# Up projections of both feed-forward stages: eight block products before, seven after

## The chip, the cores and the metric

The kernel runs on one core of a Trainium2 chip. Times are device microseconds (us); the kernel before was run three times, and its profile is one further execution. TensorE (PE) does the matrix products, VectorE (DVE), ScalarE (ACT) and GpSimd (POOL) the elementwise work, and SyncE (SP) issues the transfers. Each of them takes its instructions in order.

## The reference

One decoder layer on 512 tokens of width 1024: a feed-forward half step, a mixer of two kinds of attention, an attention into a memory, and a second feed-forward half step, each with a residual and a layer norm. The change concerns the two feed-forward stages, with weights of their own:

```
h = layer_norm(alpha*h + 0.5 * (silu(h @ w1) * (h @ w3)) @ w2)   # w1, w3: 1024 x 2816, w2: 2816 x 1024
```

Everything is float32.

## The kernel before

Tokens are kept transposed in `hT`: 1024 channels as eight contraction tiles of 128, 512 tokens along the free dimension. The 2816 hidden channels are 22 "f-tiles" of 128. An f-tile needs a piece of w1 and a piece of w3, [128, 1024] each (eight contraction tiles side by side), and for the down product a piece of w2, also [128, 1024].

A float32 operand is kept as two parts of twelve bits, `hi` and `lo`, in the type fp32r. `split` makes them: a cast gives `hi`, on ACT or DVE, whichever the planner expects to end first; a subtract on DVE, the source less `hi`, gives `lo`. Each product is then three matmuls (`mm3`, line 260): hi with hi, hi with lo, lo with hi. `project` forms one column tile of h @ w: eight contraction tiles, 24 matmuls of 512 columns into one PSUM bank.

The f-tiles form ten groups: nine of two, and the last of four. `ffn` issues the up products of group g + 1, then the down products of group g: for each of four token tiles and two halves of the output a bank `res`, which DVE adds to the accumulator `acc`. So a round of the loop is four up projections (96 matmuls) and 48 matmuls of the down product. `gated` turns two finished up banks into the gate g: silu on ACT, a multiply on DVE, and a split. The first group of the second stage goes through `project_halves`, token half by token half, since the norm before it releases the tokens in tiles; each norm is followed by PE's transposes `trh`, whose banks are split into `hT`.

Weights pass through `Weights` (from line 272): a transfer into one of three raw buffers, then a split into one of five `hl` buffers. A piece is asked for when an earlier one is done with, so the split of the piece waits until PE has read the old content of its buffer. Gates, accumulators, norm constants and other tiles of 4 KB a partition share an arena of 20 slots; there are seven work tiles [128, 512] and eight PSUM banks.

The order of the instructions is made by a planner (`Issue`): generators issue PE's instructions, and an instruction of another engine leaves when the planner's clock says that its data should be there. Splits of weights carry a delay (`LATER`, 4 us), by which they give way to others. On the chip each engine runs its queue in the order so made. In names below, `w1_1_8` is the piece of w1 for stage 1, f-tile 8; the second feed-forward stage has the number 4.

Of the kernel before, what the change touches and what calls it, by code (L numbers as in the profile page):

```python
# [10 lines left out]
F32 = mybir.dt.float32  # L11
# [7 lines left out]
P = 128  # L19
# [24 lines left out]
class Op:  # L44
    """An instruction that awaits its turn: a form for each engine that could run it."""
# [6 lines left out]
class Mark:  # L52
    """The time from which awaited data can be read; endless until it is set and the last instruction before it left."""
# [9 lines left out]
class Issue:  # L63
    """Sets the order of the instructions. Generators issue the tensor engine's; each yields what its next piece waits
    for (nothing, a Mark, or a condition), and of those that could go on the one of the highest rank does. The clock
    counts the rows of the tensor engine. The other engines' instructions are charged by their size and leave when what
    they read should be there, so that none holds up its engine's queue."""
# [46 lines left out]
    def first(self):  # L114
        """Of the pending instructions that could start soonest, the one whose data and delay say so."""
# [5 lines left out]
    def delayed(self, ns):  # L121
        """Instructions in here give way to those whose data came up to ns later, or the other way round."""
# [4 lines left out]
    def set(self, mark, *aps):  # L127
        """The mark for these tiles as they will be after what has left or is pending."""
# [33 lines left out]
def form(engine, name, op, args, kw):  # L162
    """Engine, nanoseconds on it and after it, call; then what the call writes and reads."""
# [15 lines left out]
class Timed:  # L179
    """An engine whose instructions await their turn."""  # L180
# [12 lines left out]
def layer(ctx: ExitStack, tc: tile.TileContext, a: dict, out: bass.AP):  # L193
# [20 lines left out]
    def bank(name):  # L214
        """A bank of PSUM; what still reads one that was dropped leaves first when all are taken."""
# [12 lines left out]
    def drop(*tiles):  # L228
        """Nothing issued from here on reads these banks."""
# [10 lines left out]
    def scaled(out, src, scale=None):  # L240
        """out = src * scale on ScalarE or VectorE, whichever ends first."""
# [15 lines left out]
    def matmul(ps, w, x, start, stop):  # L257
        issue.pe(lambda: nc.tensor.matmul(ps, w, x, start=start, stop=stop), ps, w, x)  # L258

    def mm3(ps, w, x, first, last):  # L260
        """(w0 + w1).T @ (x0 + x1) without the product of the two low parts, which lies below float32's last bit."""
        matmul(ps, w[0], x[0], first, False)
        matmul(ps, w[0], x[1], False, False)
        matmul(ps, w[1], x[0], False, last)
# [7 lines left out]
    class Weights:  # L272
        """Pieces of up to 1024 columns in the order of their use, as two parts of twelve bits whose sum they are;
        up to `depth` are on chip or on their way."""
# [7 lines left out]
        def fetch(self):  # L282
            key, src = self.specs.pop(0)
            n = src.shape[1]
# [25 lines left out]
    # ---------------------------------------------------------------- constants  # L310
# [19 lines left out]

    def first_loads():
        """The first weights and x, in pieces that let the products start."""
# [3 lines left out]
        for k0, k1, x0, x1 in ((0, 2, 0, 1), (2, 4, 1, 2), (4, 8, 2, 4), (8, 8, 4, 6), (8, 8, 6, 8)):  # L336
# [3 lines left out]
            raw = slot(f"xT{x0}", F32)  # L340
            raw = raw[:, :x1 - x0]
# [9 lines left out]
    def project(name, w, toks=slice(None), o=0):  # L351
        """A column tile of h @ w, transposed: [128 channels, tokens] in a bank."""
# [7 lines left out]
    def project_halves(keys, ready):  # L360
        """Column tiles of h @ w on half of the tokens, then on the other half, each when its norm is done."""
# [110 lines left out]
    def plan_ffn(n, w1, w3, w2):  # L472
# [6 lines left out]
        for g, fs in enumerate(groups):  # L479
            if g + 1 < len(groups):  # L480
                up(groups[g + 1])
# [747 lines left out]
```

## Time and profile before

| | us |
|---|---|
| median of three runs (1301.07 to 1302.55) | 1301.34 |
| profiled execution: span | 1300.1 |
| PE busy in the span | 1279.1 |
| DVE busy | 736.5 |
| ACT busy | 403.7 |
| first feed-forward stage, products from | 10.38 |
| second stage, products from | 924.08 |

The span is the profiled program from its first to its last instruction; the runs are timed from outside. The share of busy time is an average over stages with different limits, so a stage is read by its own stretch: the chain of waits, which follows the work that ended last back from the end, shows in each stretch the engine that was waited for. A matmul's mean duration in the groups is longer than the distance from one to the next, since they are pipelined; durations of DVE and ACT overlap a little too.

### The profile page before, as it was taken

What the parts mean: (1) busy time and instruction counts of PE and PEld (TensorE: products, weight loads), DVE (VectorE), ACT (ScalarE), POOL (GpSimd) and SP (SyncE); (2) the same over time, 40 slices, a digit from 0 to 9 for tenths busy, and PEclk for the clock granted to TensorE, in tenths of its full rate; (3) what the DMA queues carried; (4) which work ended last, traced back from release to release, by engine and by line L of the source; (5) the groups of instructions that cost most, each with busy time, mean ns of one, the idle gap of its engine ahead of it and who ended that gap; (6) DMA issues with size and microseconds to landing.
All of it is one profiled execution on the core that took longest, in us unless ns stands there. A gap on an engine that the chain in (4) does not pass through costs nothing.

```text
span 1300.1 us, 15614 instructions
## 1 busy us (share of the span) xinstructions
PE 1279.1 (98%) x6210; PEld 1059.8 (82%) x6210; DVE 736.5 (57%) x1250; ACT 403.7 (31%) x670; POOL 22.8 (2%) x33
## 2 busy tenths in 40 slices
PE   7999999999999999999999999999999999999997
PEld 5888887888889987877778898888988888888886
DVE  5444444354482799666657684574754444444446
ACT  3122222121133476334441253451422222222211
POOL 0000000000010000000000000000100000000000
PEclk9999999999999999999999999999999999999999
DMA  7323333243332412232333444234532232332231
GB/s 272 127 97 97 98 97 91 66 146 98 114 110 91 133 50 66 64 115 81 97 98 113 169 171 147 81 125 151 196 124 89 94 97 98 97 97 87 94 96 65
DMA packets 43212, 142.99 MB, mean 110 GB/s; under 512 B 4963, under 2 KB 6755, under 8 KB 43140
## 3 DMA queue, kind: packets, MB, share of 16 engines
q1 hardware_dynamic: 43140, 142.00, 33.6%
q8 instruction: 49, 0.80, 0.3%
q14 instruction: 23, 0.19, 0.0%
HBM read 132.94 MB, written 9.04 MB: 109 GB/s over the span
## 4 chain that ended last, share of the span: by engine, by line
PE 92%; DVE 5%; ACT 1%; DMA 1%; issue 1%; SPq 0%; POOL 0%; DVEq 0%; POOLq 0%; ACTq 0%
PE pw L258 38%; PE res_w L258 18%; PE mq L258 3%; PE res_w_o L258 3%; PE pgd L258 3%; PE res_mem_w_o L258 2%; PE mk L258 2%; PE vd L258 2%; PE qd L258 2%; PE pw_gm L258 2%; PE kd L258 2%; PE mv L258 2%; PE pyd L258 2%; PE cq L258 1%; PE pgm L258 1%; DVE ed L176 1%
## 5 line engine op out<-in xcount | busy, mean ns | idle before, releaser
L258 PE MATMUL pw<-hT,w_hl 128*128 128x512 f32 (+1 forms) x2208 | 502.5, 388 | 6.9 <-DVE w_hl L176 4.7
L258 PEld LDWEIGHTS pw<-hT,w_hl 128*128 128x128 f32 x2208 | 403.8, 189 | 101.8 <-ACT hT L176 7.5
L176 ACT CAST w_hl<-w_raw 128x1024 fp32r<-128x1024 f32 x129 | 133.5, 1050 | 514.5 <-PE pw L258 326.4
L176 DVE TENSOR_TENSOR w_hl<-w_raw,w_hl 128x1024 fp32r<-128x1024 f32 (+1 forms) x134 | 160.0, 1205 | 156.1 <-ACT w_hl L176 155.9
L258 PE MATMUL res_w<-w_hl,g 128*128 128x512 f32 x1056 | 243.3, 390 | 0.0
L258 PEld LDWEIGHTS res_w<-w_hl,g 128*128 128x128 f32 x1056 | 198.0, 188 | 41.8 <-DVE w_hl L176 0.3
L176 DVE TENSOR_TENSOR acc<-acc,res_w 128x512 f32<-128x512 f32 x128 | 85.3, 685 | 50.4 <-PE res_w L258 50.4
L176 DVE SCALAR_TENSOR_TENSOR s<-pw,s 128x512 f32<-128x512 f32 x44 | 30.4, 691 | 141.3 <-PE pw L258 140.6
L258 PE MATMUL pgd<-hT,w_gd_hl 128*128 128x512 f32 x192 | 47.5, 400 | 0.0
L258 PE MATMUL mq<-hT,mem_wq_hl 128*128 128x512 f32 x192 | 46.1, 398 | 0.0
L258 PE MATMUL res_mem_w_o<-mem_w_o_hl,moT 128*128 128x512 f32 x192 | 44.5, 391 | 0.0
L258 PE MATMUL res_w_o<-w_o_hl,zT 128*128 128x512 f32 x192 | 44.5, 391 | 0.0
L258 PEld LDWEIGHTS mq<-hT,mem_wq_hl 128*128 128x128 f32 x192 | 35.8, 188 | 8.3
L258 PEld LDWEIGHTS pgd<-hT,w_gd_hl 128*128 128x128 f32 x192 | 35.5, 188 | 8.4
L258 PEld LDWEIGHTS res_mem_w_o<-mem_w_o_hl,moT 128*128 128x128 f32 x192 | 35.8, 188 | 7.7 <-DVE mem_w_o_hl L176 0.3
L258 PEld LDWEIGHTS res_w_o<-w_o_hl,zT 128*128 128x128 f32 x192 | 35.8, 188 | 7.7 <-DVE w_o_hl L176 0.3
L176 ACT ACTIVATE s<-pw 128x512 f32<-128x512 f32 x44 | 26.0, 591 | 16.6 <-PE pw L258 16.6
L176 POOL TENSOR_TENSOR rs_ln<-ms_ln,mhalf 128x1 f32<-128x1 f32 x16 | 13.4, 836 | 997.7 <-DVE ms_ln L176 997.7
L176 DVE TENSOR_TENSOR g<-s,g 128x512 fp32r<-128x512 f32 x44 | 30.1, 684 | 0.0
L176 DVE SCALAR_TENSOR_TENSOR acc<-acc,res_w 128x512 f32<-128x512 f32 x32 | 21.6, 684 | 13.2 <-PE res_w L258 13.2
L176 ACT ACTIVATE sq<-acc,nmu 128x1024 f32<-128x1024 f32 x16 | 18.5, 1154 | 30.7 <-DVE nmu L176 29.2
L258 PE MATMUL pgm<-hT,w_gm_hl 128*128 128x512 f32 x96 | 24.9, 402 | 0.0
(243 smaller groups left out, 1397.1 us busy)
## 6 DMA issues: line engine op xcount, KB each, us to landing
w_raw<-in_ffn_w SPq DMA_DIRECT2D x131, 512.0 KB, 3.6
h_dram<-acc SPq DMA_DIRECT2D x12, 512.0 KB, 2.7
acc<-h_dram SPq DMA_DIRECT2D x12, 512.0 KB, 5.8
w_gm_raw<-in_w_gate SPq DMA_DIRECT2D x8, 512.0 KB, 3.5
w_gd_raw<-in_w_gate SPq DMA_DIRECT2D x8, 512.0 KB, 3.5
w_o_raw<-in_w_o SPq DMA_DIRECT2D x8, 512.0 KB, 3.5
mem_wk_raw<-in_mem_wk SPq DMA_DIRECT2D x8, 512.0 KB, 4.1
mem_wq_raw<-in_mem_w_q SPq DMA_DIRECT2D x8, 512.0 KB, 4.1
```

What stands on the lines that cost most here:

```text
L176: return (name, ns, 1500.0 if name == "sync" else 0.0, lambda: getattr(engine, op)(*args, **kw)), outs, ins
L258: issue.pe(lambda: nc.tensor.matmul(ps, w, x, start=start, stop=stop), ps, w, x)
```

## The change

The f-tiles 2 to 21 of each stage are taken in ten pairs, and the up projections of a pair as a product of 2 x 2 blocks: two f-tiles (f0, f1), two halves of the contraction (K0, K1) and two halves of the tokens (one, two). Each block of weights, b0 = (f0, K0), b1 = (f1, K0), b2 = (f0, K1), b3 = (f1, K1), is [128, 1024]: 512 columns of w1 and 512 of w3. `up` is hT's first half of contraction tiles, `low` its second. The seven products, in their order of issue, each with 24 matmuls of 256 columns into one bank:

```
P1 = b0 . up[one]            P5 = (b0+b1) . a           P6 = (b0+b1+b3) . b      P3 = b3 . c
P7 = (b1+b3) . (up[one]-up[two])    P2 = b2 . low[one]    P4 = (b0+b1+b3+b2) . low[two]
a = low[two]-up[two]    b = -a-up[one]    c = -b-low[one]
bank x: P1, then P6, P7, P4 on top;   bank z: P5, then P3 on top;   bank y: P2
f0[one] = P1+P2   f0[two] = x after P4   f1[one] = -(x after P6 + z)   f1[two] = -(P5 + x after P7)
```

ACT copies bank x after P1, bank z after P5 and bank x after P6 (tiles p1, p5, u2), and DVE adds to these what is still missing; the signs are taken in by the scale of silu and of the multiply. The four sums of h are split into four tiles once per stage (`sums_of_h`), two of them in the pool `ppool` that the mixer uses between the stages. The sums of weights are formed in place in the raw blocks by DVE, each before its split. Blocks now lie in the arena and come in two transfers of 256 KB. For the sums, the raw x is kept (first stage), or ACT copies the transposes of the norm's output (second stage, 16 copies). The first group of each stage goes as before; after it `ffn` waits by a mark for the sums of h.

```diff
-    def mm3(ps, w, x, first, last):
+    def mm3(ps, w, x, first, last, again=False):
...
         def fetch(self):
             key, src = self.specs.pop(0)
+            if callable(src):
+                hl = wsplit.tile([P, 2, 1024], F32R, tag="hl", name=f"{key}_hl")
+                with issue.delayed(LATER):
+                    src(hl)
+                self.tiles[key] = hl
+                self.held += 1
+                return
...
                 split(dst[:, :, 0], dst[:, :, 1], ps.rearrange("p (k t) -> p k t", k=4))
+                if n == 3:
+                    for j in range(2):
+                        act.copy(h_raw[2 * half + j][:, :, t * P:(t + 1) * P], ps[:, j * 256:(j + 1) * 256].rearrange("p (k t) -> p k t", k=2))
...
+        def load(self, *blocks):
+            for i in blocks:
+                if i not in self.b:
+                    self.b[i] = slot(f"{self.name}_b{i}", F32, [P, 1024])
+                    for w, src in enumerate(self.src):
+                        sp.dma_start(self.b[i][:, w * 512:w * 512 + 512], src[i % 2][:, i // 2 * 512:i // 2 * 512 + 512])
...
+        def make(self, i, hl):
+            b = self.b
+            if i == 1:
+                self.load(0, 1, 3, 2)
+            if self.after and i in (3, 2):
+                self.after.load(*((0, 1) if i == 3 else (3, 2)))
+            for at, other in {5: ((0, 1),), 6: ((0, 3),), 7: ((1, 3),), 4: ((0, 2),)}.get(i, ()):
+                SUM.tensor_tensor(b[at], b[at], b[other], op=ALU.add)
+            src = b[{1: 0, 5: 0, 6: 0, 4: 0, 3: 3, 7: 1, 2: 2}[i]]
+            split(hl[:, 0], hl[:, 1], src)
...
+    ORDER = (1, 5, 6, 3, 7, 2, 4)
+    SUM = dve
...
+        with issue.delayed(LATER):
+            for j in range(2):
+                up, low = h_raw[j], h_raw[2 + j]
+                kk = slice(2 * j, 2 * j + 2)
+                a, b, c = [wk(f"S{n}_{j}{i}").rearrange("p (k t) -> p k t", k=2) for i in "abc"]
+                dve.tensor_tensor(a, low[:, :, two], up[:, :, two], op=ALU.subtract)
+                split(views[0][:, kk, 0], views[0][:, kk, 1], a)
+                dve.scalar_tensor_tensor(b, a, -1.0, up[:, :, one], op0=ALU.mult, op1=ALU.subtract)
+                split(views[1][:, kk, 0], views[1][:, kk, 1], b)
+                dve.scalar_tensor_tensor(c, b, -1.0, low[:, :, one], op0=ALU.mult, op1=ALU.subtract)
+                split(views[j][:, 4:6, 0], views[j][:, 4:6, 1], c)
+                dve.tensor_tensor(a, up[:, :, one], up[:, :, two], op=ALU.subtract)
+                split(s3[j][:, :, 0], s3[j][:, :, 1], a)
...
+        def seven(p):
...
+            def product(ps, i, first):
+                hl = W.take(f"wp{n}_{p}_{i}")
+                for w in range(2):
+                    for k in range(4):
+                        o = w * 512 + k * P
+                        mm3(ps[:, w * 256:(w + 1) * 256], hl_of(hl, slice(o, o + P)), sums[i](k),
+                            first and w == 0 and k == 0, w == 1 and k == 3, not first)
+                W.done(f"wp{n}_{p}_{i}")
+
+            def out(dst, c, sign):
+                act.activation(dst, c[:, :256], AF.Silu, scale=sign)
+                dve.scalar_tensor_tensor(dst, c[:, 256:], 0.5 * sign, dst, op0=ALU.mult, op1=ALU.mult)
...
+            product(x, 1, True)
+            p1 = wk(f"p1_{n}_{p}")
+            act.copy(p1, x)
+            yield
+            z = bank(f"pz{n}_{p}")
+            product(z, 5, True)
+            p5 = wk(f"p5_{n}_{p}")
+            act.copy(p5, z)
+            yield
+            product(x, 6, False)
+            u2 = wk(f"u2_{n}_{p}")
+            act.copy(u2, x)
+            yield
+            product(z, 3, False)
+            dve.tensor_tensor(u2, u2, z, op=ALU.add)
+            drop(z)
+            out(gw[1][:, one], u2, -1.0)
+            yield
+            product(x, 7, False)
+            dve.tensor_tensor(p5, p5, x, op=ALU.add)
+            out(gw[1][:, two], p5, -1.0)
+            gT[f1] = slot(f"g{n}_{f1}")
+            split(gT[f1][:, 0], gT[f1][:, 1], gw[1])
+            yield
+            y = bank(f"py{n}_{p}")
+            product(y, 2, True)
+            dve.tensor_tensor(p1, p1, y, op=ALU.add)
...
+            product(x, 4, False)
+            out(gw[0][:, two], x, 1.0)
...
             if g + 1 < len(groups):
-                yield from up(groups[g + 1])
+                for f in groups[g + 1][::2]:
+                    yield from seven(f // 2)
             yield from down(g)
```

The change moves instructions on PE and on DVE. PE's queue in a round of the first stage, before: the up products of f-tile 8 and the start of f-tile 9 (`pw1`, `pw3` are the banks of w1 and w3, `hT0` and `hT1` the two halves of the contraction).

```order
L258 MATMUL res1_w2_1_4_3_1_893<-w2_1_5_hl_732,g1_5_627 128x512 x3
L258 MATMUL pw1_1_8_910<-hT0_89,w1_1_8_hl_762 128x512 x12
L258 MATMUL pw1_1_8_910<-hT1_90,w1_1_8_hl_762 128x512 x12
L258 MATMUL pw3_1_8_942<-hT0_89,w3_1_8_hl_798 128x512 x12
L258 MATMUL pw3_1_8_942<-hT1_90,w3_1_8_hl_798 128x512 x12
L258 MATMUL pw1_1_9_974<-hT0_89,w1_1_9_hl_828 128x512 x12
```

After, the pair of f-tiles 10 and 11 (`px`, `pz`, `py` are the banks x, z, y of pair 5; `wp1_5_6` is the block of product 6; `S1`, `S3` hold the sums of h).

```order
L258 MATMUL px1_5_1566<-hT0_89,wp1_5_1_hl_1412 128x256 x24
L258 MATMUL pz1_5_1603<-S1_0_114,wp1_5_5_hl_1444 128x256 x24
L258 MATMUL px1_5_1566<-S1_1_115,wp1_5_6_hl_1476 128x256 x24
L258 MATMUL pz1_5_1603<-S1_0_114,wp1_5_3_hl_1551 128x256 x6
L258 MATMUL pz1_5_1603<-S1_1_115,wp1_5_3_hl_1551 128x256 x6
...
L258 MATMUL px1_5_1566<-S3_1_0_116,wp1_5_7_hl_1554 128x256 x6
L258 MATMUL px1_5_1566<-S3_1_1_117,wp1_5_7_hl_1554 128x256 x6
...
L258 MATMUL py1_5_1726<-hT1_90,wp1_5_2_hl_1591 128x256 x24
L258 MATMUL px1_5_1566<-hT1_90,wp1_5_4_hl_1628 128x256 x24
```

Four projections of 24 wide matmuls became seven products of 24 narrow ones; three take tokens from `hT`, four from the tiles of sums, and bank x is written four times.

DVE's queue in a round, before: from the low parts of a piece of w3 and two of w2 to that of f-tile 12's w3 (names ending in `hl` are split weights, `raw` the loaded ones, `s` and `g` the gate).

```order
L176 TENSOR_TENSOR w3_1_11_hl_1107<-w3_1_11_raw_1106,w3_1_11_hl_1107 128x1024
L176 TENSOR_TENSOR w2_1_8_hl_1109<-w2_1_8_raw_1108,w2_1_8_hl_1109 128x1024
L176 TENSOR_TENSOR w2_1_9_hl_1144<-w2_1_9_raw_1143,w2_1_9_hl_1144 128x1024
L176 SCALAR_TENSOR_TENSOR s1_10_1178<-pw3_1_10_1148,s1_10_1178 128x512
L176 CAST g1_10_1179<-s1_10_1178 128x512
L176 TENSOR_TENSOR w1_1_12_hl_1174<-w1_1_12_raw_1173,w1_1_12_hl_1174 128x1024
L176 TENSOR_TENSOR g1_10_1179<-s1_10_1178,g1_10_1179 128x512
L176 TENSOR_TENSOR w3_1_12_hl_1210<-w3_1_12_raw_1209,w3_1_12_hl_1210 128x1024
```

After, from the end of pair 4's product 3 on (`wp1_5_b0` is pair 5's raw block b0, into which the sums go; `gw` is the gate before its split).

```order
L176 CAST wp1_5_1_hl_1412<-wp1_5_b0_1245 128x1024
L176 TENSOR_TENSOR p5_1_4_1322<-p5_1_4_1322,px1_4_1259 128x512
L176 TENSOR_TENSOR wp1_5_1_hl_1412<-wp1_5_b0_1245,wp1_5_1_hl_1412 128x1024
L176 SCALAR_TENSOR_TENSOR gw1_4_1_1258<-p5_1_4_1322,gw1_4_1_1258 128x256
L176 TENSOR_TENSOR wp1_5_b0_1245<-wp1_5_b0_1245,wp1_5_b1_1246 128x1024
L176 CAST g1_9_1413<-gw1_4_1_1258 128x512
L176 CAST wp1_5_5_hl_1444<-wp1_5_b0_1245 128x1024
L176 TENSOR_TENSOR p1_1_4_1287<-p1_1_4_1287,py1_4_1419 128x512
L176 TENSOR_TENSOR wp1_5_5_hl_1444<-wp1_5_b0_1245,wp1_5_5_hl_1444 128x1024
L176 TENSOR_TENSOR g1_9_1413<-gw1_4_1_1258,g1_9_1413 128x512
L176 TENSOR_TENSOR wp1_5_b0_1245<-wp1_5_b0_1245,wp1_5_b3_1285 128x1024
L176 SCALAR_TENSOR_TENSOR gw1_4_0_1257<-p1_1_4_1287,gw1_4_0_1257 128x256
```

The gate of one pair and the weight blocks of the next now alternate instruction by instruction, and casts and additions of 1024 stand among the subtracts.

PE's queue where the second stage begins, before (`trh3_3` are the transposes of the last token tile, `pw1_4_0` the first bank of the stage).

```order
L258 MATMUL pw3_4_0_7585<-hT0_89,w3_4_0_hl_7547 128x256 x12
L258 MATMUL pw3_4_0_7585<-hT1_90,w3_4_0_hl_7547 128x256 x12
L258 MATMUL pw1_4_1_7586<-hT0_89,w1_4_1_hl_7549 128x256 x12
L258 MATMUL pw1_4_1_7586<-hT1_90,w1_4_1_hl_7549 128x256 x12
L258 MATMUL pw3_4_1_7587<-hT0_89,w3_4_1_hl_7551 128x256 x12
L267 MATMUL trh3_3_0_7685<-ident_84,acc3_3_7227 128x128 x4
L267 MATMUL trh3_3_1_7690<-ident_84,acc3_3_7227 128x128 x4
```

After, at the same place.

```order
L258 MATMUL pw3_4_0_8650<-hT0_89,w3_4_0_hl_8602 128x256 x12
L258 MATMUL pw3_4_0_8650<-hT1_90,w3_4_0_hl_8602 128x256 x12
L258 MATMUL pw1_4_1_8651<-hT0_89,w1_4_1_hl_8604 128x256 x12
L267 MATMUL trh3_3_0_8729<-ident_84,acc3_3_8270 128x128 x4
L267 MATMUL trh3_3_1_8734<-ident_84,acc3_3_8270 128x128 x4
```

The transposes moved ahead of 24 of the 84 matmuls that stood before them.

DVE's queue there, after (`S4_0` and so on are the sums of h of that stage, `hraw` the raw transposes; `w1_4_1` belongs to the first group, which goes as before).

```order
L176 TENSOR_TENSOR wp4_1_b1_8609<-wp4_1_b1_8609,wp4_1_b3_8610 128x1024
L176 CAST wp4_1_5_hl_8809<-wp4_1_b0_8608 128x1024
L176 TENSOR_TENSOR S4_0a_8907<-hraw2_8407,hraw0_8405 128x512
L176 TENSOR_TENSOR wp4_1_5_hl_8809<-wp4_1_b0_8608,wp4_1_5_hl_8809 128x1024
L176 TENSOR_TENSOR S4_1a_8910<-hraw3_8408,hraw1_8406 128x512
L176 TENSOR_TENSOR wp4_1_b0_8608<-wp4_1_b0_8608,wp4_1_b3_8610 128x1024
L176 SCALAR_TENSOR_TENSOR s4_0_8899<-pw3_4_0_8650,s4_0_8899 128x512
L176 CAST wp4_1_6_hl_8837<-wp4_1_b0_8608 128x1024
L176 TENSOR_TENSOR S4_0_8903<-S4_0a_8907,S4_0_8903 128x2x256
```

The sums of h, the blocks of the first pair and the gates of the first group now stand in one queue there, where before the low part of a piece of w3 was followed by the gate.

## Rows read from the trace of the kernel before

**Rows 1.** The page: span, busy time by engine, granted clock, the chain by engine.

```profile
span 1300.1 us, 15614 instructions
...
PE 1279.1 (98%) x6210; PEld 1059.8 (82%) x6210; DVE 736.5 (57%) x1250; ACT 403.7 (31%) x670; POOL 22.8 (2%) x33
...
PEclk9999999999999999999999999999999999999999
...
PE 92%; DVE 5%; ACT 1%; DMA 1%; issue 1%; SPq 0%; POOL 0%; DVEq 0%; POOLq 0%; ACTq 0%
```

**Rows 2.** Chain of waits in order of time, first stage (start us, us, what).

```profile
10.38 45.69 PE pw L258 x186
...
100.34 22.49 PE pw L258 x96
122.83 10.89 PE res_w L258 x48
```

**Rows 3.** Windows: busy time of each engine in a stretch; the first line names the columns.

```profile
core 0: us, PE busy (x) PEld busy (x) DVE busy (x) ACT busy (x) POOL busy (x), PEclk, DMA share, GB/s
133.70:167.10 33.40, 33.40 (x146) 27.11 (x145) 15.69 (x20) 7.21 (x9) 0.00 (x0) 1.00 0.31 95
...
935.70:969.10 33.40, 33.40 (x194) 29.17 (x193) 14.08 (x18) 10.66 (x12) 0.00 (x0) 1.00 0.44 149
```

**Rows 4.** TensorE's groups by form: up matmuls, weight loads (name, count | busy us, mean ns | idle).

```profile
L258 PE MATMUL pw<-hT,w_hl 128*128 128x512 f32 x2016 | 479.5, 398 | 6.9 <-DVE w_hl L176 4.7 <-ACT hT L176 1.9 <-DVE hT L176 0.3
...
L258 PEld LDWEIGHTS pw<-hT,w_hl 128*128 128x128 f32 x2208 | 403.8, 189 | 101.8 <-ACT hT L176 7.5 <-DVE hT L176 1.7 <-issue 0.5
```

**Rows 5.** Chain of waits: stretches of 256-column matmuls.

```profile
769.95 14.39 PE mk L258 x120
...
924.08 9.86 PE pw L258 x84
...
934.82 35.31 PE pw L258 x204
```

**Rows 6.** Timeline of VectorE in the round from 133.7 us (start us, us, instruction).

```profile
145.80 0.43 DVE L176 CAST g<-s 128x512 fp32r<-128x512 f32 x1
146.14 1.22 DVE L176 TENSOR_TENSOR w_hl<-w_raw,w_hl 128x1024 fp32r<-128x1024 f32 x1
147.28 0.68 DVE L176 TENSOR_TENSOR g<-s,g 128x512 fp32r<-128x512 f32 x1
...
159.12 1.91 DVE L176 TENSOR_TENSOR acc<-acc,res_w 128x512 f32<-128x512 f32 x3
161.70 0.69 DVE L176 TENSOR_TENSOR acc<-acc,res_w 128x512 f32<-128x512 f32 x1 [0.67 <-PE res_w L258]
```

**Rows 7.** VectorE's groups by form.

```profile
L176 DVE TENSOR_TENSOR w_hl<-w_raw,w_hl 128x1024 fp32r<-128x1024 f32 x131 | 158.5, 1220 | 156.0 <-ACT w_hl L176 155.9
...
L176 DVE TENSOR_TENSOR on<-on,od 128x256 f32<-128x256 f32 x8 | 3.4, 419 | 3.5 <-ACT on L176 3.4
...
L176 DVE CAST w_hl<-w_raw 128x1024 fp32r<-128x1024 f32 x2 | 1.4, 690 | 4.2 <-PE pw L258 4.2
```

**Rows 8.** ScalarE's groups by form.

```profile
L176 ACT CAST w_hl<-w_raw 128x1024 fp32r<-128x1024 f32 x129 | 133.5, 1050 | 514.5 <-PE pw L258 326.4 <-DVE acc L176 119.1 <-PE res_w L258 31.4
L176 ACT ACTIVATE s<-pw 128x512 f32<-128x512 f32 x44 | 26.0, 591 | 16.6 <-PE pw L258 16.6
...
L176 ACT COPY on<-od 128x256 f32<-128x256 f32 x6 | 2.2, 370 | 7.5 <-PE od L258 7.5
```

**Rows 9.** VectorE's timeline at the entrances of both stages.

```profile
14.81 1.22 DVE L176 TENSOR_TENSOR w_hl<-w_raw,w_hl 128x1024 fp32r<-128x1024 f32 x1
...
931.22 1.28 DVE L176 SCALAR_TENSOR_TENSOR acc<-u,rs_ln,lnb 128x1024 f32<-128x1024 f32 x1 [0.44 <-POOL rs_ln L176]
...
940.21 1.22 DVE L176 TENSOR_TENSOR w_hl<-w_raw,w_hl 128x1024 fp32r<-128x1024 f32 x1 [3.89 <-ACT w_hl L176]
```

**Rows 10.** GpSimd's timeline before the second stage.

```profile
928.65 2.53 POOL L176 TENSOR_TENSOR rs_ln<-ms_ln,mhalf 128x1 f32<-128x1 f32 x1 [8.24 <-DVE ms_ln L176]
```

More of the change, by code (lines that the diff above doesn't have):

```diff
@@ L255, in split, with matmul @@
             dve.scalar_tensor_tensor(lo, src, scale, f32(hi), op0=ALU.mult, op1=ALU.subtract)
[L257 to L264 removed]
+    def matmul(ps, w, x, start, stop, again=False):
+        issue.pe(lambda: nc.tensor.matmul(ps, w, x, start=start, stop=stop, skip_group_check=again), ps, w, x)
+    def mm3(ps, w, x, first, last, again=False):
+        matmul(ps, w[0], x[0], first, False, again)
+        matmul(ps, w[0], x[1], False, False, again)
+        matmul(ps, w[1], x[0], False, last, again)
     def transpose(ps, src):
@@ new lines, in layer, with sums_of_h @@
+    ORDER = (1, 5, 6, 3, 7, 2, 4)
+    SUM = dve
+    def sums_of_h(n, sums):
+        pts = [ppool.tile([P, 2, 13, P], F32R, tag="pt", name=f"S{n}_{i}").rearrange("p a b c -> p (a b c)") for i in range(2)]
+        views = [t[:, :3072].rearrange("p (k i t) -> p k i t", k=6, i=2) for t in pts]
+        s3 = [slot(f"S3_{n}_{i}") .rearrange("p k (i t) -> p k i t", i=2) for i in range(2)]
+        sums[5] = lambda k: [views[0][:, k, i] for i in (0, 1)]
+        sums[6] = lambda k: [views[1][:, k, i] for i in (0, 1)]
+        sums[3] = lambda k: [views[k // 2][:, 4 + k % 2, i] for i in (0, 1)]
+        sums[7] = lambda k: [s3[k // 2][:, k % 2, i] for i in (0, 1)]
+        one, two = slice(0, 256), slice(256, 512)
+        with issue.delayed(LATER):
[11 more added lines that the diff above has]
+                split(s3[j][:, :, 0], s3[j][:, :, 1], a)
+        mark = issue.when(views[0], views[1], s3[0], s3[1])
+        h_raw.clear()
+        for i, (k0, toks) in {1: (0, one), 2: (4, one), 4: (4, two)}.items():
+            sums[i] = lambda k, k0=k0, toks=toks: hk(k0 + k, toks)
+        return mark
@@ L479, in plan_ffn @@
+    def plan_ffn(n, w1, w3, w2):
+        for f in groups[0]:
+            W.plan(f"w1_{n}_{f}", w1[f])
+            W.plan(f"w3_{n}_{f}", w3[f])
+        pairs = [Pair(f"wp{n}_{p}", [w[2 * p:2 * p + 2] for w in (w1, w3)]) for p in range(1, NF // 2)]
+        for p, q in zip(pairs, pairs[1:]):
+            p.after = q
         for g, fs in enumerate(groups):
             if g + 1 < len(groups):
-                up(groups[g + 1])
+                for f in groups[g + 1][::2]:
+                    pairs[f // 2 - 1].plan()
@@ L486, in ffn @@
         res = Residual(n, src)
-        gT = {}
+        gT, sums = {}, {}
         def gated(f, pa, pb):
@@ L505, in up @@
                 gated(f, *ps)
+        def seven(p):
+            x, y, z = None, None, None
+            def product(ps, i, first):
[9 more added lines that the diff above has]
+                dve.scalar_tensor_tensor(dst, c[:, 256:], 0.5 * sign, dst, op0=ALU.mult, op1=ALU.mult)
+            one, two = slice(0, 256), slice(256, 512)
+            gw = [wk(f"gw{n}_{p}_{i}") for i in range(2)]
+            f0, f1 = 2 * p, 2 * p + 1
+            x = bank(f"px{n}_{p}")
+            product(x, 1, True)
[25 more added lines that the diff above has]
+            dve.tensor_tensor(p1, p1, y, op=ALU.add)
+            drop(y)
+            out(gw[0][:, one], p1, 1.0)
+            yield
+            product(x, 4, False)
+            out(gw[0][:, two], x, 1.0)
+            drop(x)
+            gT[f0] = slot(f"g{n}_{f0}")
+            split(gT[f0][:, 0], gT[f0][:, 1], gw[0])
+            yield
         def down(g):
@@ L520, in ffn @@
             if g + 1 < len(groups):
-                yield from up(groups[g + 1])
+                for f in groups[g + 1][::2]:
+                    yield from seven(f // 2)
             yield from down(g)
@@ L983, in out_proj @@
         for m in sizes:
+            if n == 3 and k0 + m == KT:
+                h_raw.extend(slot(f"hraw{j}", F32) for j in range(4))
             if n == 2 and k0 + m == KT:
```

23 lines of the change are left out of this document (16 added, 7 removed).

## Prediction

> **What bounds the kernel now.** I began with the page's busy line. TensorE (PE) is busy 1279.1 of the 1300.1 us span, VectorE (DVE) 736.5, ScalarE (ACT) 403.7; the granted clock is full, 2.4 GHz, in every slice; and 92% of the chain of waits is PE's own work [rows 1]. In the feed-forward stages the kernel takes as long as PE's products take, so a change there counts in full as long as nothing else comes to be waited for.
>
> Next I followed the chain through one round of the first feed-forward stage: the up products of a pair of f-tiles (96 matmuls of 512 columns, 22.49 us), then 48 matmuls of the down product (10.89 us) [rows 2]. A round is 33.4 us, and PE has no gap in it while DVE works 15.69 us [rows 3]. The spacing is 22.49/96 = 234.3 ns for an up matmul and 10.89/48 = 226.9 for a down one. The mean duration of one in the groups, 398 ns, is not its price, because matmuls overlap [rows 4]; I use the chain's time divided by its count throughout.
>
> **What goes from TensorE.** A pair now takes seven products, each of two projections, four contraction tiles and three matmuls, 24 in all, of 256 columns: 168 matmuls for 96 of twice the width. What does a matmul of 256 columns cost? Two stretches of before have them back to back: 9.86/84 = 117.4 ns with the tokens taken from hT, 14.39/120 = 119.9 with a smaller tile [rows 5]. Three of the seven products (1, 2, 4) move columns of hT and four move the new sums, so a pair takes 72 x 0.1174 + 96 x 0.120 = 19.97 us. That saves 2.52 us a pair and, for ten pairs in each of two stages, 50.3 us. All at 117.4 would be 55.3; all at 120.0, 46.6.
>
> A rule speaks against this. The mean weight load lasts 189 ns [rows 4], longer than the 117 ns between two matmuls of 256 columns [rows 5]; so in this trace loads overlap each other or are recorded with their wait, and no fixed part shows: half the columns take half the time. The Trainium skill (TensorE: Matmul & The Clock Gate, Back-to-back issue gap) says that load and matmul together set the spacing, about 81 ns at 128 columns and 131 at 512. By a straight line between these, an estimate, 256 columns would take 98 ns; 168 x 98 - 96 x 131 ns = 3.9 us more a pair, 78 us more in all. The trace does not agree: it has 234 at 512 and 117 at 256 [rows 2, 5]. The form of this that rows can price is the third rival.
>
> **What is added on VectorE.** Per round, before: six low-part subtracts of weights, eight accumulations, two each of gate multiply, cast and subtract. After: nine low-part subtracts (seven blocks, two w2), four block additions of the same shape, four casts of 1024 that the order gives to DVE, eight accumulations, three additions of 512 (p1, p5, u2), four gate multiplies of 256, one cast and two subtracts of g. I price each by the distance between starts when DVE is not waiting, since successive records overlap: 1.14 us for 1024 elements with two inputs (146.14 to 147.28), 0.34 for a cast of 512 (145.80 to 146.14), 0.61 for an accumulation of 512, where three in a row take 1.91 and the last of them 0.69 [rows 6]. Casts of 1024 are recorded at 0.690, an addition of 256 at 0.419, each 0.08 more than the step [rows 7], so 0.61 and 0.34. The round is 13 x 1.14 + 4 x 0.61 + 0.34 + 8 x 0.61 + 3 x 0.61 + 4 x 0.34 + 2 x 0.61 = 26.9 us. With the full records (1.220, 0.690, 0.43, 0.69, 0.419, 0.68) it is 29.7. PE's new round is 19.97 + 10.89 = 30.9. DVE stays under it either way, by 4 us or 1.2. I take 26.9, since most of these instructions have another ready behind them. DVE's busy time should rise from 736 to about 1020 us (20 x 13.2 and the sums of h).
>
> ACT loses a cast of 1024 a round (1.05 us) and gains three copies of 512 (up to 0.59, the price of an activation of that size) and, for two activations of 512, four of 256 (a copy of 256 takes 0.37) [rows 8]: from 7.2 us [rows 3] to some 9 a round, at most 12. PE's round covers it. The weight blocks bring the same bytes as before in twice as many transfers, a round earlier than needed.
>
> **Does each part arrive in time?** Let a round start with product 1 at 0, each product 2.85 us. From DVE's order with the steps above, low parts are done and needed at: block 3, 2.4 and 8.55; block 7, 3.5 and 11.4; block 2, 6.4 and 14.25; block 4, 8.25 and 17.1. The three copies of banks that PE goes on to write are due at 5.7, 8.55 and 11.4, and done at about 4.5, 6.4 and 10.25; the last addition that frees bank x (p5) at 15.6, needed at 17.1. The tightest stretch runs from the end of product 7 to the next round's block 3: 20 DVE instructions, 16.7 us, in 17.8 us, with 6 us more before PE needs block 3. So I expect no steady wait; the bound from below is 0, from above the first rival's.
>
> **The two entrances.** In the first stage the sums of h (subtracts and casts of x) stand ahead of a weight piece on DVE, where before the low part at 14.81 followed hT directly [rows 9]. I expect 1 us there and 0.4 at product 5: +1.5 us, from 0 (hidden under the first 45.69 us of products [rows 2]) to 12, the sum of the 20 or so new DVE instructions at 0.61.
>
> In the second stage two things move. First, the transposes of the last token tile stand after 60 up matmuls, not 84. They need the tile's norm, whose last product ran 931.22 to 932.50 [rows 9] behind a POOL power of 2.53 us [rows 10]. PE arrives at 924.08 + 60 x 0.1174 = 931.1 [rows 5], so it waits up to 1.4 us; one weight subtract fewer stands ahead of the norm there, so I take 1.0. Second, on DVE the cast of block 5 waits for PE's last use of its buffer (about 939), and behind it stand all the sums of h, the two gates and the blocks of the first pair. Before, DVE took its next piece at 940.21 and was busy for 14.08 of the 33.4 us from 935.7 [rows 3, 9]. PE finishes the first f-tiles at 934.82 [rows 5] + 108 x 0.1174 = 947.5 and would begin product 4 at 964.6. Counting the order's rows down to block 4's low part at the steps above, it is there at 969.3: +4.7 us. Together +5.7, with bounds 3 and 16 (nothing hidden behind the 12 us of sums).
>
> **The sum**, against the profiled execution: 1300.1 - 50.3 + 1.5 + 5.7 = 1257.0 us of span. The median of the runs, 1301.3, lies 1.2 above the span; so 1258 us.
>
> **Rivals.**
> *VectorE becomes the bound (slower).* At full records, 29.7, plus the waits of an accumulation for its bank, 0.67 each and six a round [rows 6], which no other work fills if the order is too strict, DVE's round is 33.7 against 33.4 before. Nothing is saved, 20 x 0.3 and the entrances' 7.2 are added: 1301.3 + 13.2 = 1314.5. For it: DVE would be busy more than 85% of a round, and its work stands in one queue behind bank releases. Against: in before those waits stand where DVE has nothing else to do. It decides from a DVE round of 30.9, 4 us above my count; below 33 the gain is only partly lost. Chance 0.08.
> *Partial waits or a dear entrance.* Half the gain lost to waits of about 1.2 us a pair, or both entrances at their upper bounds (12 and 16): 1258 + 20 to 25 = 1278 to 1283; milder, 1268 up. For it: the second entrance's queue is long. Against: the slack of 4 us a round. Chance 0.14.
> *A matmul has a fixed part.* If a weight load of 189 ns [rows 4] bounds each matmul's step, a pair takes 168 x 0.189 = 31.8 us for 22.49: +186, 1487 us. Against it, the 117 ns of 84 matmuls in a row. Chance 0.03.
> *The change doesn't do what it says* (no gain, no loss, within 0.2%, about what a measurement of this kernel can tell): if waits eat just what is saved. Chance 0.03.
>
> **How the numbers follow.** My forecast holds 0.72, within 1249 to 1268 (PE's products at 117.4 and no entrance cost is 1246; all at 120 and entrances at 16 is 1271). The second rival's lower part brings the upper end to 1276; beyond it and below 1249 I leave two in ten. Faster: 0.72 + 0.14 and a little of the first rival's partial form, 0.87; same 0.03; slower, the first and third, 0.10.
>
> **What would show it.** In the new profile: a pair's seven products near 20.0 us and 117 to 120 ns a matmul; rounds near 30.9; DVE near 1020 us busy and still idle for some us in each down product; PE idle 4 to 6 us at the second stage's first pair and hardly elsewhere. The forecast is wrong if rounds exceed 31.5 with PE waiting for DVE's weight parts, p5 or u2, or if a matmul of the sums takes over 125 ns.

## The result, and the profile after

The changed kernel takes 1262.57 us (median of four runs, 1260.29 to 1263.87) against 1301.56 before: a ratio of 0.9699, with a 95% interval of 0.9685 to 0.9712. The forecast was 1258 us, range 1249 to 1276. The profiled execution has a span of 1261.3 us, where the sum in the prediction gave 1257.0: 38.8 us went in place of 43.1.

The page after, the four lines that answer to [rows 1]:

```profile
span 1261.3 us, 19011 instructions
...
PE 1234.5 (98%) x7650; PEld 1101.9 (87%) x7650; DVE 984.8 (78%) x1577; ACT 453.2 (36%) x807; POOL 21.7 (2%) x33
...
PEclk9999999999999999999999999999989999999999
...
PE 90%; DVE 7%; ACT 1%; issue 1%; DMA 1%; SPq 0%; POOL 0%; DVEq 0%; POOLq 0%; ACTq 0%
```

PE is still busy for 98% of the span and makes up 90% of the chain: it bounds the kernel as before. DVE's busy time rose from 736.5 to 984.8 us (1020 was expected). One digit of the clock line is no longer 9; it is the stretch at the second stage's entrance, below.

One round, in the chain of waits (start us, us, what); it answers to [rows 2]:

```profile
96.78 2.85 PE px L258 x24
99.63 2.87 PE pz L258 x24
...
111.15 2.82 PE py L258 x24
...
116.78 10.93 PE res_w L258 x48
```

The next round starts at 127.71: 30.93 us, where the prediction had 30.9 and before 33.38. Products that move hT take 2.82 us (117.4 ns a matmul; 2.85 for the first of a round), those that move sums 2.88 (120.0). All seven make 20.00 us; the forecast was 19.97.

Busy time by engine in that round, at the second entrance, and just after it; columns as in [rows 3]:

```profile
96.78:127.71 30.93, 30.93 (x218) 29.01 (x218) 27.26 (x36) 8.76 (x14) 0.00 (x0) 1.00 0.31 103
911.20:935.05 23.85, 20.97 (x173) 20.36 (x171) 21.29 (x29) 12.41 (x21) 0.00 (x0) 0.98 0.52 193
935.05:951.10 16.05, 16.05 (x110) 15.89 (x111) 13.97 (x18) 3.58 (x6) 0.00 (x0) 0.82 0.27 83
```

In the steady round PE has no gap and DVE is busy 27.26 us (26.9 was worked out), so 3.7 us are free. At the entrance PE loses 2.9 us, and in the 16 us after it the granted clock is 0.82. The timeline of PE there (`px` x7 and x8 are product 6, `pz` x7 and x17 product 5, `py` product 2; in a steady round PE's queue has them one after the other, here they stand interleaved):

```profile
929.59 0.99 PE L258 MATMUL pz<-S,wp_hl 128*128 128x256 f32 x7
930.89 0.50 PE L258 MATMUL py<-hT,wp_hl 128*128 128x256 f32 x2 [0.31 <-ACT wp_hl L176]
932.93 1.09 PE L258 MATMUL px<-S,wp_hl 128*128 128x256 f32 x7 [1.54 <-ACT p L176]
935.05 2.07 PE L258 MATMUL px<-S,wp_hl 128*128 128x256 f32 x8 [1.03 <-DVE S L176]
936.92 3.83 PE L258 MATMUL pz<-S,wp_hl 128*128 128x256 f32 x17
940.55 1.31 PE L258 MATMUL px<-S,wp_hl 128*128 128x256 f32 x9
```

PE waits 0.31, 1.54 and 1.03 us, for the cast of block 2, for the copy p1 and for a sum of h. After that 25 matmuls take from 935.05 to the start of the last row, 5.5 us, where at 120 ns they would take 3.0. The granted clock of just this stretch is 0.50: these matmuls run at the lower of the clock's two levels, 1.2 GHz. The chain's steps return to 2.88 us per 24 from 941.9 on. DVE in the same stretch:

```profile
918.40 0.69 DVE L176 CAST wp_hl<-wp_b 128x1024 fp32r<-128x1024 f32 x1 [2.53 <-PE pw L258]
...
934.31 0.69 DVE L176 TENSOR_TENSOR S<-S_1b,S 128x512 fp32r<-128x512 f32 x1
```

The first of these rows is the cast of block 5, held until PE has left its buffer, as predicted; the second is the low part of sum b, which product 6 needs. Between them DVE has no gap: 16 us of sums, blocks and gates in one queue. The copy p1 is ACT's and starts at 932.30, behind four casts in ACT's queue: of block 2, of a gate and two of the sums.

The third place where time went is one that the prediction did not have. SP's timeline in the first stage (start us, us from the first issue to the last, count), then DVE's, beginning with the first cast of the next pair in a steady round, and PE's:

```profile
204.71 0.89 SPq L176 DMA_DIRECT2D wp_b<-in_ffn_w  x2
219.95 0.80 SPq L176 DMA_DIRECT2D bias_dram<-rows  x1
220.80 18.51 SPq L176 DMA_DIRECT2D wp_b<-in_ffn_w  x14
```

```profile
111.18 0.69 DVE L176 CAST wp_hl<-wp_b 128x1024 fp32r<-128x1024 f32 x1 [0.24 <-PE px L258]
...
247.40 0.69 DVE L176 TENSOR_TENSOR acc<-acc,res_w 128x512 f32<-128x512 f32 x1 [0.67 <-PE res_w L258]
249.37 0.69 DVE L176 CAST wp_hl<-wp_b 128x1024 fp32r<-128x1024 f32 x1
```

```profile
256.25 2.88 PE L258 MATMUL pz<-S,wp_hl 128*128 128x256 f32 x22 [0.36 <-DVE wp_hl L176]
259.82 0.47 PE L258 MATMUL px<-S,wp_hl 128*128 128x256 f32 x2 [0.68 <-ACT p L176]
```

SP issues the first two of the eight transfers of pair 8's blocks at 204.71 and then stands until 219.95 before the store of the bias table, which waits for its rows; the other six and the eight of pair 9 are queued behind it. DVE takes its first block of pair 8 at 249.37, after idling between accumulations from 243 on, and pair 8's products then wait for casts and copies. In a steady round that cast starts 5.6 us before the down product (111.18 and 116.78); here it comes 7.5 us after the down product's start (241.88).

Late data alone don't explain this. By the trace the first block landed at 209.3 us and the last of pair 8 at 239.0, before a steady round's casts and sums would have asked for them (from 236.3 and 239.0 on). At 249.37 the cast waits for nothing; it stands in DVE's queue behind five accumulations, each of which waits for PE. The fourth experiment changes the store's place and this order together, so why the order came out so, no run shows.

From the start of the down product in which the table is made (209.40) to that of the last but one (326.28) it is 116.9 us; with the table elsewhere (fourth experiment) 112.7. Without the 1.2 us of the table's own matmuls 3.0 us were lost, against 0.3 in the same place before the change: 2.6 us more.

### The profile page after: what moved, and what is told of

It is laid out like the page before. It is cut to its first block, busy times and chain, and to the rows that moved or that the text cites. A ratio compares the mean times of both kernels' runs of the same rounds, so it can differ in the third digit from the quotient of the medians.

```text
span 1261.3 us, 19011 instructions
## 1 busy us (share of the span) xinstructions
PE 1234.5 (98%) x7650; PEld 1101.9 (87%) x7650; DVE 984.8 (78%) x1577; ACT 453.2 (36%) x807; POOL 21.7 (2%) x33
## 4 chain that ended last, share of the span: by engine, by line
PE 90%; DVE 7%; ACT 1%; issue 1%; DMA 1%; SPq 0%; POOL 0%; DVEq 0%; POOLq 0%; ACTq 0%
PE res_w L258 19%; PE px L258 18%; PE pz L258 9%; PE py L258 4%; PE mq L258 4%; PE res_w_o L258 3%; PE res_mem_w_o L258 3%; PE pgd L258 3%; PE pw L258 3%; PE mk L258 2%; PE vd L258 2%; PE pw_gm L258 2%; PE qd L258 2%; PE kd L258 2%; PE mv L258 2%; PE pyd L258 2%
## 5 line engine op out<-in xcount | busy, mean ns | idle before, releaser
L258 PEld LDWEIGHTS res_w<-w_hl,g 128*128 128x128 f32 x1056 | 196.6, 188 | 40.8 <-issue 0.5
L176 DVE TENSOR_TENSOR wp_hl<-wp_b,wp_hl 128x1024 fp32r<-128x1024 f32 x140 | 169.2, 1220 | 8.5 <-ACT wp_hl L176 7.8
L258 PE MATMUL px<-S,wp_hl 128*128 128x256 f32 x960 | 123.5, 285 | 3.5 <-ACT p L176 2.2
L258 PE MATMUL pz<-S,wp_hl 128*128 128x256 f32 x960 | 124.0, 285 | 0.8 <-ACT wp_hl L176 0.5
L258 PEld LDWEIGHTS px<-S,wp_hl 128*128 128x128 f32 x960 | 119.2, 193 | 4.2 <-ACT p L176 2.6
L258 PEld LDWEIGHTS pz<-S,wp_hl 128*128 128x128 f32 x960 | 119.8, 194 | 1.2 <-ACT wp_hl L176 0.7
L258 PE MATMUL px<-hT,wp_hl 128*128 128x256 f32 x960 | 119.5, 280 | 0.0
L258 PEld LDWEIGHTS px<-hT,wp_hl 128*128 128x128 f32 x960 | 117.3, 188 | 1.6 <-DVE p L176 0.2
L176 DVE TENSOR_TENSOR wp_b<-wp_b,wp_b 128x1024 f32<-128x1024 f32 x80 | 97.4, 1218 | 0.1
L176 ACT CAST w_hl<-w_raw 128x1024 fp32r<-128x1024 f32 x47 | 49.1, 1048 | 83.7 <-PE px L258 37.2
L258 PEld LDWEIGHTS pw<-hT,w_hl 128*128 128x128 f32 x288 | 43.1, 197 | 13.7 <-ACT hT L176 7.7
```

Source lines behind the costliest of these rows:

```text
L176: return (name, ns, 1500.0 if name == "sync" else 0.0, lambda: getattr(engine, op)(*args, **kw)), outs, ins
```

## The experiments

Each kernel is the changed one with the edit shown, cut short; the first two share one edit. Ratios are to the kernel before, with 95% intervals.

**One stage alone.** `by_seven` decides which pairs go by seven products; the others go through `up` as before, and a stage without pairs makes no sums of h.

```diff
-                for f in groups[g + 1][::2]:
-                    yield from seven(f // 2)
+                for f in groups[g + 1][::2]:
+                    if by_seven(n, f // 2):      # n == 1 alone, or n == 4 alone
+                        yield from seven(f // 2)
+                    else:
+                        yield from up([f, f + 1])
```

> Seven products in the first stage alone; the second stage as before, without its sums of h and copies. Theory (PE's saving less three separate costs, read from the changed kernel's trace): 10 pairs x 2.45 us less 1.4 at the stage's start and 2.6 where the bias table is made = 20.5 us less than before, 1281 us, and no drop of the granted clock anywhere. Rival (the shortfall of 4 us against the forecast is spread evenly, PE a little slower all through): half of the whole gain, 19.5 us; then the stretch from 241.9 to 286.5 us would not be longer than other rounds.

> Seven products in the second stage alone; the first as before. Theory: 10 x 2.45 us less 6.2 at the stage's entrance = 18.3 us less than before, 1283 us; the trace shows the waits of 0.3, 1.5 and 1.0 us and the granted clock below 1 at that entrance, as in the changed kernel, and the bias table costs under 0.3 us. Rival (even spread): 19.5 us, 1282, and no stretch that stands out.

Measured: 1279.79 us (0.9833, 0.982 to 0.9847) and 1282.53 (0.9852, 0.9839 to 0.9866), so 21.8 and 19.0 us less than before where 20.5 and 18.3 were expected, and the first gains more than the second, against the even spread. Together they make 40.8, a little more than the 39.0 of both. Pair 8 waits at the bias table in the first kernel (0.36, 0.68 and 0.47 us, as in the changed one); in the second that stretch is as before. In the second, PE waited at the entrance as in the changed kernel, but the clock did not fall, which was expected wrongly; its chain there:

```profile
955.08 1.22 PE px L258 x8
956.31 2.04 PE pz L258 x17
```

The same 17 matmuls took 2.04 us and not the 3.63 between the starts at 936.92 and 940.55. So the waits come with the order of the instructions, and the drop of the clock after them does not come in every execution. The one profiled here was the fastest of its four, 1280.31 us, at a mean granted clock of 0.998; the other three have 0.996 to 0.997.

**The second stage's first pair by eight products.**

```diff
+                    if by_seven(n, f // 2):      # n == 1 or p > 1, p the pair
```

> The changed kernel with the first pair of the second stage (f-tiles 2 and 3) by eight products as before, so that the sums of h and the first blocks have one more round to be made in. Theory (the entrance costs 6.2 us because the sums, the blocks of the first pair and the gates stand in one DVE queue; PE waits 2.9 us for them and then runs some 5 us at the lower clock): the wait and the clock drop go, the pair's 2.5 us of gain goes too: 1259 us (1258 to 1260.5). Rival (the cost is in the copies of the transposes and the transposes that moved ahead): 6.2 us stay and 2.5 are lost: 1265 us.

Measured: 1258.49 us (0.9672, 0.9659 to 0.9686), as the theory had it. The chain at the entrance has no wait any more:

```profile
910.02 37.99 PE pw L258 x228
948.01 10.89 PE res_w L258 x48
```

The stretch from the stage's first up matmul to the start of the second round's down product, 76.9 us, is what before had (79.5) less the 2.45 of one pair; in the changed kernel it was 80.7 with two pairs shorter. The entrance thus cost 80.7 - (79.5 - 4.9) = 6.1 us in that execution. In the second experiment's, with the same waits and the clock full, the stretch is 78.3 us, so 3.7; in the fourth experiment's, where the clock fell for a shorter time, 79.7, so 5.1.

**The bias table late.**

```diff
         consts()
+        later = Mark()
+        later.floor = 312000.0
+        yield later
         bias_table()
```

The table is then made before the last down product of the stage.

> The changed kernel with the bias table and lambda made before the last down product of the first stage in place of its middle. Theory (the store of the bias table waits 14 us in SP's queue for its rows, and the weight blocks queued behind it land late, so that DVE is idle and then late): the 2.6 us lost between 241.9 and 286.5 us go, 1260 us, and the rounds there take 30.9 us. Rival (the cost goes wherever the tables go: PE's and ACT's own part, the table load of ACT): 1262.6, no change.

Measured: 1260.39 us (0.9683, 0.967 to 0.9696). The rounds there are 30.93 us; two starts of down products show it:

```profile
240.54 10.93 PE res_w L258 x48
271.47 10.93 PE res_w L258 x48
```

In the medians the gain is 2.2 us, in the trace 2.7 (the stage ends at 358.86 in place of 361.59). The median alone could not tell 2.2 from run to run (the changed kernel's runs differ by 3.6); the rows do. They show that the table's place makes the loss; moving it also gave the blocks' casts back their steady place in DVE's order, so the run doesn't tell late transfers from late casts.

**The sums laid out as hT is.** The four tiles of sums take rows of 512 columns, hi and lo a row apart, two products sharing a row.

```diff
-        views = [t[:, :3072].rearrange("p (k i t) -> p k i t", k=6, i=2) for t in pts]
+        views = [t[:, :3072].rearrange("p (b i t) -> p b i t", b=3, i=2) for t in pts]
...
-        sums[5] = lambda k: [views[0][:, k, i] for i in (0, 1)]
+        sums[5] = lambda k: [views[k // 2][:, k % 2, i, one] for i in (0, 1)]
```

> The changed kernel with the sums of h laid out as hT is (hi and lo rows of 512, products 5 and 6 taking the halves of one row, 3 and 7 of another), four more small casts and subtracts per stage for it. Theory (the 120.0 ns of a matmul that moves sums, against 117.4 for hT, comes from how the rows lie): the four products drop from 2.88 to 2.82 us, 5 us in all, less about 0.5 at the entrances: 1258 us. Rival (it is not the layout): 120.0 stays, 1263 us.

Measured: 1259.65 us (0.9675, 0.9662 to 0.9688), a time near the theory's for another reason. A product with sums still takes 2.88 us:

```profile
101.42 2.88 PE px L258 x24
```

What fell is the entrance: the casts and subtracts of the sums came in another order, and from the stage's first up matmul to the second round's down product it took 76.7 us, not 80.7. A time that fits a theory does not show it; the rows of the step it speaks of do.

**More work for DVE.** The low-part subtract of some blocks is done twice, with the same result: of two blocks, of five, of all seven.

```diff
             split(hl[:, 0], hl[:, 1], src)
+            if i in (1, 2):      # (1, 5, 3, 7, 2) in the second kernel, all in the third
+                dve.tensor_tensor(hl[:, 1], src, f32(hl[:, 0]), op=ALU.subtract)
```

> The changed kernel with the low-part subtract of blocks 1 and 2 done twice: two more DVE instructions of 1.14 us a pair. Theory (a round has 30.93 - 27.26 = 3.7 us of DVE idle time, so DVE is not on the path): rounds stay at 30.9 us; with up to 2.3 us more in the queue of the second entrance 1263 to 1266 us. Rival (DVE is already part of the bound): 20 x 2.3 us more, 1308 us, rounds of 33.2.

> The same with blocks 1, 5, 3, 7 and 2 done twice: five more, 5.7 us a pair. Theory: DVE's round becomes 27.26 + 5.7 = 33.0 us, above PE's 30.9, so DVE bounds the round: some 18 rounds x 2.0 and 5 us at the entrances, 1302 us (1298 to 1308), DVE busy without a gap and PE waiting for it in each round. Rival (DVE's waits do not shrink): 20 x 5.7 more, 1377 us. Rival (more slack than the trace shows): under 1270 us.

> Every block's low-part subtract twice: seven more DVE instructions of 1.14 us a pair. With five more the planner gave the blocks' casts to ACT (36 of the first stage's on DVE became 6), DVE's round was 30.2 us and PE's stayed at 30.93. There are no casts left to move now. Theory (DVE bounds the round as soon as its own work exceeds PE's): DVE's round is 20 x 1.14 + 0.3 + 8 x 0.61 + 3 x 0.61 + 4 x 0.34 + 2 x 0.61 = 32.4 us, 1.5 above PE's; some 18 rounds x 1.5 and 12 us at entrances and ends, 1300 us (1292 to 1308), rounds of 32.4 in the trace with DVE busy throughout. Rival (DVE's waits for banks stay, 4 us a round, and are not filled): rounds of 36, 1370 us. Rival (it still hides): 1275 us, rounds of 30.9.

Measured: 1260.68 us (0.9684, 0.9671 to 0.9697), 1272.79 (0.9779, 0.9766 to 0.9792) and 1317.02 (1.012, 1.01 to 1.014). With two more, rounds stay at 30.93 us, with DVE busy 28.13 and ACT 11.38; the time lies below the 1263 to 1266 that was expected, and the runs don't tell it from the changed kernel's. Windows of one round with five more and with seven more, and PE's timeline in the latter:

```profile
99.50:130.43 30.93, 30.93 (x219) 29.01 (x218) 30.09 (x37) 12.77 (x18) 0.00 (x0) 1.00 0.31 103
```

```profile
133.12:166.21 33.09, 31.50 (x219) 29.16 (x218) 33.03 (x40) 12.85 (x18) 0.00 (x0) 1.00 0.28 96
```

```profile
144.30 1.42 PE L258 MATMUL res_w<-w_hl,g 128*128 128x512 f32 x5 [1.39 <-ACT w_hl L176]
```

With five more the expectation of 33.0 us was wrong: the planner moved the casts of blocks from DVE to ACT (ACT is busy 12.77 us in place of 8.76), DVE's round became 30.1 and PE's stayed at 30.93; the 10 us came at the entrances and the last two pairs. With seven more nothing was left to move: rounds of 33.1 us with DVE busy for all but 0.1 (0.5 in the next), PE waiting, and the whole kernel 1.2% slower than before. The wait shown ends with a cast on ACT, which is busy 12.85 us only; that DVE holds the round is read from the window, not from this row. 32.4 was worked out for the round, 1300 for the time; the excess is in these rounds and at the entrances. So the prediction's first rival was a real one, and its point of decision lies where it was put, as far as two runs can say: a DVE round of 30.1 costs nothing in a steady round, one of 33.0 bounds it.

**The sums of blocks on GpSimd.**

```diff
-    SUM = dve
+    SUM = pool
```

The planner's price for a GpSimd instruction of this size was set to 2 ns an element with it.

> The changed kernel with the four block additions of each pair on GpSimd in place of DVE. DVE's round falls by 4 x 1.14 = 4.6 us. Theory (DVE is not on the path in steady rounds): nothing is gained there, rounds stay at 30.93; at the second entrance two or three additions leave DVE's queue, up to 3 us less: 1260 to 1263 us if GpSimd keeps up. Rival (GpSimd and DVE slow each other, as GpSimd's power of 0.55 us took 2.53 beside DVE's subtracts; blocks come late): rounds above 31 and over 1270 us.

Measured: 1281.4 us (0.9845, 0.9829 to 0.9862). The groups of GpSimd and DVE, then a steady round:

```profile
L176 POOL TENSOR_TENSOR wp_b<-wp_b,wp_b 128x1024 f32<-128x1024 f32 x80 | 201.4, 2518 | 419.7 <-DVE wp_hl L176 275.6 <-DMA w_raw<-in_ffn_w 99.1 <-PE py L258 39.6
```

```profile
L176 DVE CAST g<-gw 128x512 fp32r<-128x512 f32 x40 | 73.5, 1838 | 1.1
L176 DVE TENSOR_TENSOR g<-gw,g 128x512 fp32r<-128x512 f32 x40 | 54.2, 1354 | 0.6
```

```profile
102.04:132.97 30.93, 30.93 (x218) 29.01 (x218) 27.29 (x31) 10.13 (x15) 9.86 (x5) 1.00 0.31 103
```

Both theories hold in part. Steady rounds are the same 30.93 us, so DVE is not on the path there. But DVE has won nothing: four additions of 1.14 us left it, and its round is still 27.29, since its casts of g take 1838 ns in place of 421 in the changed kernel and the subtracts of g 1354 in place of 685, beside additions of 2518. The 19 us were lost where there is no slack, at the starts, at the bias table (pair 8's stretch is 40 us) and in the last pairs. The Trainium skill (SBUF — State Buffer, Who interferes with whom) says that DVE and GpSimd share a pair of ports as an exclusive lock, which DVE's casts can take and of which an instruction with two inputs in SBUF needs the reading side. The stretched casts and subtracts of g agree. DVE's block subtracts are hardly longer (1266 ns, 1220 before); that they seldom stand beside an addition, since the next one into their block has to wait for them, is argued from the kernel and not tested.

**Without the sums of h.** Products 5, 6, 3 and 7 take columns of hT.

```diff
-                split(views[0][:, kk, 0], views[0][:, kk, 1], a)
...
+        for i, (k0, toks) in {1: (0, one), 2: (4, one), 4: (4, two), 5: (0, two), 6: (0, one), 3: (4, one), 7: (0, two)}.items():
```

> The changed kernel without the sums of h: products 5, 6, 3 and 7 take columns of hT as they are (the sums, their casts and subtracts are left out; the raw copies, the sums of weights and everything else stay). It tells two things apart. The matmul: if 120.0 ns against 117.4 belongs to the moving tile, all seven products take 2.82 to 2.85 us and 20 x 0.25 = 5 us go; if it belongs to these products or their place in the round, 120.0 stays. The entrance: if the sums in DVE's queue make its cost (theory), the waits at the second stage's first pair go, 5 us, and about 1 us at the first stage: 1251 to 1253 us in all; if the blocks and gates alone are late (rival), the waits there stay and the time is 1257 to 1258.

Measured: 1250.72 us (0.961, 0.9597 to 0.9623). The chain in a steady round and at the second entrance:

```profile
98.77 2.85 PE pz L258 x24
110.16 2.85 PE py L258 x24
```

```profile
923.06 2.85 PE px L258 x24
925.91 2.85 PE pz L258 x24
```

The entrance: its waits are gone, and the stretch that was 80.7 us is 74.9, within 0.3 of what two pairs should leave. So nearly all of its 6.1 us is the sums of h in the queues of DVE and ACT, with the clock after them. The matmul: every product now takes 2.85 us, 118.7 ns, neither 117.4 nor 120.0. Seven take 19.93 us in place of 20.00, 1.4 us in all and not 5. Even a product whose tokens come from hT in both kernels (2, in `py`) went from 2.82 to 2.85 us, so the price doesn't belong to the moving tile alone; why stays open.

The time is 11.9 us below the changed kernel's, more than these two make. The bias table's loss is gone as well, though its store is in the same place of the stage. SP's timeline:

```profile
203.50 4.50 SPq L176 DMA_DIRECT2D wp_b<-in_ffn_w  x8
221.93 0.80 SPq L176 DMA_DIRECT2D bias_dram<-rows  x1
```

All eight transfers of pair 8 now stand ahead of the store, and pair 8's round is 30.84 us like the others. That fits the reading that the loss needs blocks queued behind the store.

**Both mends at once.**

The two edits together.

> The changed kernel with the first pair of the second stage by eight products and the bias table late, both at once. If the two losses are separate, the gains add: 1262.6 - 4.1 - 2.2 = 1256.3 us, no wait of PE over 0.5 us for the sums, the gates or the blocks in either stage. If one hides the other, 1258.5 us as with the first alone.

Measured: 1255.83 us (0.9649, 0.9636 to 0.9662). The gains add (1256.3 was expected), and of the kernels that leave nothing out it is the fastest. The window of 46 us about its second entrance, PE without a gap and the clock full:

```profile
899.00:945.00 46.00, 46.00 (x303) 41.72 (x302) 37.73 (x53) 23.27 (x38) 1.63 (x1) 1.00 0.76 263
```

## Why the prediction was right

**The seven products.** 22.49 - 19.97 was forecast, 22.49 - 20.00 measured; the down product rose from 10.89 to 10.93. So 2.45 us a pair and 49.0 in all, 1.3 less than the 50.3 of the sum. The bounds, 117.4 and 120.0 ns, both appeared, on the tiles that they were taken for, though the kernel without sums shows that they are not the tiles' own. The Trainium skill's spacing (TensorE: Matmul & The Clock Gate, Back-to-back issue gap), from which the prediction's estimate was 3.9 us more a pair, is not what these rows show: half the columns took half the time again.

**VectorE beside it.** 26.9 us a round was forecast, 27.26 measured, and no steady round has a wait. This was the step on which the sign hung, and the added subtracts put a price on it: it held with 3.7 us free, and a DVE round of 33 makes the kernel slower than before. Its price for this case, 1314.5 us at a round of 33.7, is near the 1317.0 measured at rounds of 33. What the prediction lacked is that the planner balances the casts between DVE and ACT, which gives some 3 us more (33.0 expected with five more, 30.1 measured). The busy total came out 35 us under the forecast, which had put 13.2 us a pair into it; its own figures give 26.9 - 15.69 = 11.2, the windows of a round 27.26 - 15.69 = 11.6, and 20 x 1.6 is the difference, nearly.

**The entrances.** +1.5 forecast at the first, 1.2 measured, partly by luck. PE's rows there:

```profile
10.50 23.86 PE L258 MATMUL pw<-hT,w_hl 128*128 128x512 f32 x90 [2.08 <-ACT hT L176]
...
38.39 0.51 PE L258 MATMUL py<-hT,wp_hl 128*128 128x256 f32 x2 [0.35 <-ACT wp_hl L176]
```

The wait of 0.35 costs 0.6 us with what follows it, near the 0.4 put at product 5. The other 0.6 us are not the sums ahead of a weight piece, put at 1: the 90 matmuls have no wait among them. They take 23.7 us where the first 90 took 23.0 before, since steps of 0.43 us, the lower clock, last until 15.7 us and not until 14.1. In the profiles of the first and third experiments, whose first stage has the same code, the second down product starts 1.8 and 1.1 us earlier.

+5.7 at the second, 6.1 measured. The place and the cause (the sums queued behind block 5's cast) were right; the price was put together otherwise. Product 4, which the walk had late by 4.7 us, is not what waited; product 6 was, for p1 and for a sum, and two matmuls of product 2 before it, 2.9 us together; another 2.5 came from the lower clock after these waits, of which the prediction knew nothing. The wait at the moved transposes, put at 1.0, did not come. So here too the sum was nearer than its terms: without the clock it is 3.7.

**The bias table.** This is the step that failed: "So I expect no steady wait". The walk through DVE's order took the blocks as present and one round for all. In pair 8's round the store of the bias table stands in SP's queue ahead of six of the pair's eight transfers, DVE's queue has the pair's first cast 13 us later than in other rounds, and the 2.6 us lost there are most of the 4.3 that the sum is short. The terms measured, 49.0 - 1.2 - 6.1 - 2.6 = 39.1, leave 0.3 of the 38.8 unexplained.

## What to carry to other kernels

Trading matrix work for elementwise work pays as long as the elementwise engine's own round, added up from the distances between starts, stays under the matrix engine's; here the margin was 12%, and past it the change turns into a loss. The costs that remain sit at the seams: where a stage begins with its sums to make, and where a store that waits for data stands among the loads in the one queue that issues both. Giving the first unit of work after a seam the old way can win more than it loses.

## What the runs showed of the hardware

After PE's waits of 0.3, 1.5 and 1.0 us the granted clock fell to 1.2 GHz in the changed kernel's profiled execution and not in that of the second stage alone, with the same order of instructions and the same waits: 25 matmuls took 5.5 us in the one and 3.1 in the other, and the stretch about them 80.7 and 78.3. A difference of a few us between runs of one kernel can be this.

A DVE cast of 512 elements took up to 2.5 us while GpSimd added blocks, 1.84 on average and 0.42 without, so moving work there freed nothing.
